# Two heads of an attention group side by side on TensorE: row tiles for the scores, column tiles for the value products

## The chip, the core and the metric

The kernel runs on one core of a Trainium2 chip. The metric is the device time of one execution in microseconds (us). The kernel before took 1734.57 us (median of three runs, 1733.45 to 1736.35).

## What is computed

Two layers of a diffusion trunk work on 128 context tokens and 512 latent tokens (a grid of 8 rows by 64 columns), 640 tokens of width 1024. Of a layer, this is the part that matters here:

```python
q, k, v = heads(da), heads(mla), heads(na)        # 4 heads of 64 per group
# differential attention (da):  p = softmax(q1 k1) - lam * softmax(q2 k2);  o = p v
# latent attention (mla):       p = softmax(q k / sqrt(96));                o = p v
# neighbourhood attention (na): a latent query sees 8 x 16 neighbours (bias rpb) and 128 context keys
s_loc = where(col_ok, q kb * scale + bias, -inf);  s_ctx = q kc * scale
p = softmax(concat(s_loc, s_ctx));                 o = p_loc vb + p_ctx vc
mixed = concat(o_da, o_mla, o_na, o_conv) @ w_out
x = x + g1 * mixed;   x = x + g2 * (relu(h @ w_ff1) ** 2 @ w_ff2)
```

Latent tokens read the 128 cached context keys and their own; context tokens read only themselves. The context's keys and values are outputs as well.

## The kernel before

The large products run as three fp32r products of split operands (`mm3`, lines 244 to 246: high by high, high by low, low by high). A weight granule of 512 KB comes in on the queue of SP (L214), and ACT and POOL split it (L192, L193). The attention itself runs in plain f32 on TensorE, where the trace shows two records (passes) for each matmul.

The attention of a layer is a pipeline of 60 units in the order neighbourhood, differential, latent: 20 units each, a unit being one head and one tile of 128 queries (four latent tiles i = 0 to 3 and the context tile i = 4). `PROGRAM` sets the stages of a unit: at step t its scores (`Sa`) and the row maximum (`ma`); two steps on the transposes of the probabilities (`T`, L686) and their copy to SBUF (`ev`, L692), after the exponential (`xa`) and the division by the row sum (`sc`) one step earlier or in the same step; three steps on the value products (`PV`, L697) and their split into high and low (`oc`, L192 and L193). Between the steps stand background pieces (`mm3` of the coming projections and of the output projection), spread by a list of first and last steps. A tile scheduler then fixes the order of each engine.

Neighbourhood units went head by head (h = 0 to 3, five tiles each). A head has 64 channels, and a pair of heads fills the 128 partitions of `q` and `k`: the scores of one unit use 64 partitions, three blocks of 128 keys (L756 to L758) or one (L750, the context tile). `u["s_"]` and `u["t"]` lie in one of three PSUM slots of 1024 f32 (`s`). The bias of a head has three tables of 128 x 384; each has its buffer, and the table of the next head is loaded behind the last use of this head's (L734).

The value products took the values of both heads of a pair as weights (128 columns) for each unit, and `o_split` kept the 64 output partitions of the unit's own head. The turned probabilities `pt` have two buffers of 2560 bytes a partition. `o` lies in one of two PSUM banks (`g`), which the background pieces use too.

Of the kernel before, what the change touches and what calls it, by code (L numbers as in the profile page):

```python
# [16 lines left out]
T = 640  # L17
# [65 lines left out]
class Builder:  # L83
# [462 lines left out]
    def v(self, name):  # L546
        return self.A("va" if name == "na" else "vb", 0, 6, 256)
# [140 lines left out]
    def turn_out(self, u):  # L688
        self.pti += 1
        n = u["nb"] * 128  # L690
        u["pt"] = self.A("pt", 2560 * (self.pti % 2), n)
        self.nc.scalar.copy(u["pt"], u["t"][:, 0:n])  # L692

    def pv(self, u, p, vals):
        u["o"] = self.g()[:, 0:128]
        for b, v in enumerate(vals):
            self.nc.tensor.matmul(u["o"], v[:, p * 128:p * 128 + 128] if v.shape[1] > 128 else v, u["pt"][:, b * 128:b * 128 + 128],  # L697
                                  start=b == 0, stop=b == len(vals) - 1)
# [5 lines left out]
    def o_split(self, u, h, i):  # L704
# [25 lines left out]
    def na_bias(self, kind):  # L730
        return self.F("e", 8192 + 1536 * kind, 384)

    def na_bias_load(self, l, h, kind):
        self.nc.sync.dma_start(self.na_bias(kind), self.d["nab"][l, h, kind])  # L734

    def na_unit(self, l, h, i, orow):
        nc = self.nc
        p, r0 = h // 2, 64 * (h % 2)
        rows = slice(r0, r0 + 64)
        q = self.qk_q("na", p)[rows, i * 128:i * 128 + 128]  # L740
        k = self.qk_k("na", p)[rows]
        v = self.v("na")
        nk = 128 if i == 4 else 384
        u = {"nb": nk // 128}

        def S():
            sl = self.slot()
            u["s_"], u["t"] = sl[:, 0:nk], sl[:, 640:1024]
            if i == 4:
                nc.tensor.matmul(sl[:, 0:128], q, k[:, 640:768], start=True, stop=True)  # L750
                return
            nxt, prv = 128 * min(i + 1, 3), 128 * max(i, 1) - 64
            step = abs(prv - nxt)
            lo = min(nxt, prv)
            pair = k[:, lo:lo + 2 * step].rearrange("p (a b) -> p a b", b=step)[:, ::-1 if prv < nxt else 1, 0:64]
            nc.tensor.matmul(sl[:, 0:128], q, pair, start=True, stop=True)  # L756
            nc.tensor.matmul(sl[:, 128:256], q, k[:, i * 128:i * 128 + 128], start=True, stop=True)
            nc.tensor.matmul(sl[:, 256:384], q, k[:, 512:640], start=True, stop=True)  # L758

        def mx():  # L760
            m = u["m"] = self.small()
            if i == 4:
                nc.vector.tensor_reduce(out=m, in_=u["s_"], axis=AX.X, op=ALU.max, negate=True)
            else:
                kind = (0, 1, 1, 2)[i]
                nc.vector.tensor_tensor_reduce(out=u["s_"], in0=u["s_"], in1=self.na_bias(kind), scale=-1.0,
                                               scalar=3e38, op0=ALU.add, op1=ALU.min, accum_out=m)
                if i != 1 and h < 3:
                    self.na_bias_load(l, h + 1, kind)

        def ex():
            s = u["s"] = self.small()
            u["e"] = self.F("e", 1536 * ((h * 5 + i) % 4), nk)
            nc.scalar.activation(u["e"], u["s_"], AF.Exp, bias=u["m"], scale=1.0 if i == 4 else -1.0, accum_out=s)

        return {
            "Sa": S, "ma": mx, "xa": ex, "sc": lambda: self.softmax_row(u, ROWS[l]), "T": lambda: self.turn(u),
            "ev": lambda: self.turn_out(u),
            "PV": lambda: self.pv(u, p, [v[:, 5]] if i == 4 else [self.edge(p)[:, i], v[:, i], v[:, 4]]),
            "oc": lambda: self.o_split(u, h, i),  # L780
        }

    def mla_unit(self, l, h, i, orow):
# [5 lines left out]
        u = {"nb": nk // 128}  # L789
# [19 lines left out]
        return {  # L809
            "Sa": S, "ma": mx, "xa": ex, "sc": lambda: self.softmax_row(u, ROWS[2 + l]), "T": lambda: self.turn(u),  # L810
            "ev": lambda: self.turn_out(u),
            "PV": lambda: self.pv(u, h // 2, [v[:, 5]] if i == 4 else [v[:, j] for j in range(5)]),
            "oc": lambda: self.o_split(u, h, i),
        }

    def stk(self, mm):
# [30 lines left out]
    def da_unit(self, l, h, i, orow):  # L847
        nc = self.nc
        v = self.v("da")
        st = [self.stk(2 * (h % 2) + c) for c in range(2)]  # L850
        nk = 128 if i == 4 else T
        sq = self.F("sq", 40 * (h // 2 % 2), 5, 2)
        u = {"nb": nk // 128}

        def S(c):
            if c == 0:
# [18 lines left out]
        def sc():  # L875
# [16 lines left out]
            "oc": lambda: self.o_copy(u, h, i, orow),  # L892
        }

    def pipeline(self, l, hooks):
        self.ei = 2
        order = [(self.na_unit, h, i) for h in range(4) for i in range(5)]
        order += [(self.da_unit, h, i) for h in range(4) for i in range(5)]
        order += [(self.mla_unit, h, i) for i in (0, 1, 2, 4, 3) for h in range(4)]
        rows = [self.F("conv", 5120 + 2560 * p, T) for p in range(2)]  # L900
        n = len(order)
        units = []
        depth = max(int(p[-1]) for p in PROGRAM if p != "|")
        for t in range(n + depth):
            if t < n:
                make, h, i = order[t]
                units.append(make(l, h, i, rows[h // 2]))
# [12 lines left out]
            if t in hooks:  # L920
                hooks[t]()
# [482 lines left out]
    def mix(self, l):  # L1404
        nc, d = self.nc, self.d
# [5 lines left out]
            self.in_conv(l, self.lead)  # L1411
        self.swap(l, "bt")
        self.lam(l)
        for kind in range(3):
            self.na_bias_load(l, 0, kind)
# [280 lines left out]
```

## Time and profile before

| what | value |
|---|---|
| median of three runs | 1734.57 us |
| the profiled execution, its own time | 1735.52 us |
| its span in the trace | 1733.6 us |
| TensorE (PE) busy | 1664.6 us, 96% |
| VectorE (DVE) busy | 1083.0 us, 62% |
| ScalarE (ACT) busy | 740.7 us, 43% |
| GpSimd (POOL) busy | 656.5 us, 38% |
| mean granted TensorE clock | 0.986 |

Busy shares are means over stages with different limits, so the page is read by stages. In layer 0 the neighbourhood units lie at about 156 to 262 us, the differential ones at 262 to 338, the latent ones at 338 to 405; layer 1 has the same at about 992 to 1105, 1105 to 1181 and 1181 to 1248. The time of a matmul on the busy line is its latency; what it costs a full engine is the step from its start to the next start, and that is read from the timeline.

### The profile page before, as it was taken

Reading aid. Unit: us, or ns where it says so; the run is one execution under the profiler, and the core shown is the slowest. Engines: PE = TensorE matmul, PEld = TensorE weight load, DVE = VectorE, ACT = ScalarE, POOL = GpSimd, SP = SyncE. Lnnn points to the kernel's source line nnn. Section 1 sums busy time; section 2 is a strip of 40 time slices with the busy share of each in tenths; the row PEclk is TensorE's granted clock in tenths of the full one; section 3 lists DMA queues with packets and bytes.
Section 4 is the critical chain, followed back from the end, with each engine's and each line's share of the span. In section 5 each row is a group of like instructions: output and inputs, shape, how many; then the busy total and the mean of one; then the engine's idle time right before and its main releaser. Section 6 shows DMA issues by size and latency. Waiting matters only on the chain. (4 is left out here: it accounts for less than half of the span.)

```text
span 1733.6 us, 29318 instructions
## 1 busy us (share of the span) xinstructions
PE 1664.6 (96%) x11368; PEld 1570.3 (91%) x11368; DVE 1083.0 (62%) x2136; ACT 740.7 (43%) x1655; POOL 656.5 (38%) x527
## 2 busy tenths in 40 slices
PE   7999999999989999999999899999999999999997
PEld 5869988788889999999999888887989999999997
DVE  4772448868988887876377933886784333333335
ACT  4323666756423332222343247776563322332322
POOL 0225533305344455544324364332343333333330
PEclk8999999999989999999999999999999999999999
DMA  9563244202355454443222222430113222222221
GB/s 367 185 202 106 75 110 101 63 14 86 110 160 167 147 158 147 152 153 111 73 71 71 64 86 84 108 88 20 50 39 97 73 74 74 80 79 74 74 62 61
DMA packets 62331, 178.28 MB, mean 103 GB/s; under 512 B 8656, under 2 KB 20048, under 8 KB 62192
## 3 DMA queue, kind: packets, MB, share of 16 engines
q1 hardware_dynamic: 61984, 176.14, 33.0%
q8 instruction: 89, 1.46, 0.3%
q14 instruction: 50, 0.41, 0.1%
q10 hardware_dynamic: 144, 0.13, 0.0%
q0 software_dynamic: 64, 0.14, 0.0%
HBM read 158.52 MB, written 3.83 MB: 94 GB/s over the span
## 5 line engine op out<-in xcount | busy, mean ns | idle before, releaser
L193 POOL TENSOR_TENSOR ra<-fa,ra 128x512 fp32r<-128x512 f32 (+1 forms) x239 | 345.7, 1459 | 545.2 <-ACT ra L192 524.5
L193 POOL TENSOR_TENSOR we<-fa,we 128x512 fp32r<-128x512 f32 x126 | 188.8, 1510 | 275.2 <-ACT we L192 253.5
L1077 DVE TENSOR_TENSOR fr<-fr 128x384 f32<-128x384 f32 (+1 forms) x128 | 103.9, 814 | 273.7 <-ACT or L1076 150.6
L192 ACT CAST ra<-fa 128x512 fp32r<-128x512 f32 (+1 forms) x240 | 147.2, 621 | 255.1 <-PE s L245 163.7
L244 PE MATMUL s<-ra 128*128 128x256 f32 (+2 forms) x600 | 185.4, 309 | 8.3 <-DVE fa L392 7.6
L245 PE MATMUL s<-ra 128*128 128x256 f32 (+2 forms) x600 | 184.3, 307 | 0.0
L246 PE MATMUL s<-ra 128*128 128x256 f32 (+2 forms) x600 | 184.1, 307 | 0.0
L301 DVE CUSTOM_DVE_ANT_0 fa<-fa 128x1024 f32<-128x1024 f32 x112 | 173.2, 1546 | 0.2
L392 DVE SCALAR_TENSOR_TENSOR fa<-s,fa 128x128 f32<-128x128 f32 (+1 forms) x310 | 121.3, 427 | 74.8 <-PE s L246 74.8
L246 PE MATMUL g<-ra 128*128 128x384 f32 (+2 forms) x508 | 158.3, 312 | 8.7 <-POOL ra L193 8.7
L244 PE MATMUL g<-ra 128*128 128x384 f32 (+2 forms) x508 | 162.2, 319 | 2.5 <-DVE bt L1010 1.9
L245 PE MATMUL s<-ra,we 128*128 128x384 f32 (+1 forms) x480 | 152.1, 317 | 12.0 <-DVE ra L370 12.0
L245 PE MATMUL g<-ra 128*128 128x384 f32 (+2 forms) x508 | 157.8, 311 | 0.8 <-POOL ra L193 0.8
L192 ACT CAST we<-fa 128x512 fp32r<-128x512 f32 x132 | 81.2, 620 | 175.2 <-PE s L245 127.9
L246 PE MATMUL s<-ra,we 128*128 128x384 f32 (+1 forms) x480 | 150.1, 313 | 0.0
L244 PE MATMUL s<-ra,we 128*128 128x384 f32 (+1 forms) x480 | 148.8, 314 | 0.8 <-DVE fa L520 0.8
L392 DVE SCALAR_TENSOR_TENSOR fa<-g,fa 128x128 f32<-128x128 f32 (+1 forms) x266 | 109.3, 441 | 40.4 <-PE g L246 39.0
L244 PEld LDWEIGHTS s<-ra 128*128 128x128 f32 x600 | 115.6, 193 | 17.6 <-DVE fa L392 7.9
L423 DVE SCALAR_TENSOR_TENSOR fa<-fa 128x670 f32<-128x670 f32 x120 | 124.1, 1098 | 0.5
L697 PE MATMUL g<-at 128*128 128x128 f32 x848 | 116.9, 277 | 2.8 <-DVE fa L392 1.5
L245 PEld LDWEIGHTS s<-ra 128*128 128x128 f32 x600 | 115.9, 193 | 4.0 <-issue 4.0
L246 PEld LDWEIGHTS s<-ra 128*128 128x128 f32 x600 | 115.8, 193 | 3.6 <-issue 3.6
(299 smaller groups left out, 4484.4 us busy)
## 6 DMA issues: line engine op xcount, KB each, us to landing
fa<-in_wg SPq DMA_DIRECT2D x187, 512.0 KB, 3.6
fa<-in_wmod SPq DMA_DIRECT2D x73, 512.0 KB, 4.2
at<-in_wmod SPq DMA_DIRECT2D x20, 512.0 KB, 6.5
ra<-ra SPq DMA_DIRECT2D x64, 96.0 KB, 2.2
ra<-ra SPq DMA_DIRECT2D x64, 80.0 KB, 2.3
fa<-in_nab SPq DMA_DIRECT2D x24, 192.0 KB, 3.7
fa<-in_xT SPq DMA_DIRECT2D x8, 320.0 KB, 5.9
os<-in_wmod SPq DMA_DIRECT2D x3, 512.0 KB, 10.2
```

The source lines that it names most:

```text
L192: nc.scalar.copy(hi, src)
L193: (lo_eng or nc.gpsimd).tensor_tensor(out=lo, in0=src, in1=hi.bitcast(F32), op=ALU.subtract)
L244: nc.tensor.matmul(out, a[0], b[0], start=start, stop=False)
L245: nc.tensor.matmul(out, a[0], b[1], start=False, stop=False)
L246: nc.tensor.matmul(out, a[1], b[0], start=False, stop=stop)
L301: self.nc.vector.tensor_tensor_reduce(out=self.junk, in0=slot, in1=self.cb[:, v], scale=1.0, scalar=0.0, op0=ALU.mult, op1=ALU.add, accum_ ...
L392: self.mark = nc.vector.scalar_tensor_tensor(out=xs, in0=ps[:, a - t0:b - t0], scalar=self.mod(l, v, which)[:, m:m + 1], in1=xs, op0=ALU.m ...
L423: nc.vector.scalar_tensor_tensor(out=y, in0=g[:, j:j + 670], scalar=dwh[:, c, j:j + 1], in1=y, op0=ALU.mult, op1=ALU.add)
L697: self.nc.tensor.matmul(u["o"], v[:, p * 128:p * 128 + 128] if v.shape[1] > 128 else v, u["pt"][:, b * 128:b * 128 + 128], start=b == 0, s ...
L1077: nc.vector.tensor_tensor(out=r, in0=r, in1=r, op=ALU.mult)
```

## The change

Units of neighbourhood attention now come in pairs of heads for each query tile. At the first unit of a pair the scores of both heads are issued, block by block and head by head, the heads on partitions 0 to 63 and 64 to 127 and into the two banks of one slot. The second unit issues none. In neighbourhood and latent attention the value products of both heads are issued at the second unit (`pv2`): 64 weight columns each, one head into output partitions 0 to 63, the other into 64 to 127 of one bank. Differential attention keeps `pv`. `o_split` runs once for a pair, on 128 partitions. The turned probabilities have three buffers (1536 bytes for neighbourhood units, 2560 for the others; the third of those lies over the edge values and a scratch row). The bias tables are read in the order of the pairs (number n = 0 to 11 for a layer) through the same three buffers, and table n + 3 is loaded behind the last use of table n.

```diff
-        u["pt"] = self.A("pt", 2560 * (self.pti % 2), n)
+        u["pt"] = self.A("pt", u["size"] * ((self.pti + 2) % 3), n)
...
+    def pv2(self, u):
+
+        u["o"] = self.g()[:, 0:128]
+        pair = (u["mate"], u)
+        for b in range(u["nb"]):
+            for c, w in enumerate(pair):
+                self.nc.tensor.matmul(u["o"][64 * c:64 * c + 64], w["v"](b), w["pt"][:, b * 128:b * 128 + 128],
+                                      start=b == 0, stop=b == u["nb"] - 1)
...
-        r, c = slice(64 * (h % 2), 64 * (h % 2) + 64), slice(i * 128, i * 128 + 128)
-        hi, lo = (self.R("ob", off, 2, T)[r, h // 2, c] for off in (0, 5120))
-        self.split(hi, lo, u["o"][r], self.nc.vector)
+        c = slice(i * 128, i * 128 + 128)
+        hi, lo = (self.R("ob", off, 2, T)[:, p, c] for off in (0, 5120))
+        self.split(hi, lo, u["o"], self.nc.vector)
...
+    def na_bias_load(self, l, n):
+        if n < 12:
+            self.nc.sync.dma_start(self.na_bias(n), self.d["nab"][l, n // 6 * 2 + n % 2, n // 2 % 3])
...
+            for b in range(nk // 128):
+                for r in range(2):
+                    rows = slice(64 * r, 64 * r + 64)
+                    q, k = self.qk_q("na", p)[rows, i * 128:i * 128 + 128], self.qk_k("na", p)[rows]
...
+                    at = 512 * r + 128 * b
+                    nc.tensor.matmul(sl[:, at:at + 128], q, k, start=True, stop=True)
...
-                if i != 1 and h < 3:
-                    self.na_bias_load(l, h + 1, kind)
+                if i != 1:
+                    self.na_bias_load(l, bias + 3)
...
-        order = [(self.na_unit, h, i) for h in range(4) for i in range(5)]
+        order = [(self.na_unit, 2 * p + c, i) for p in range(2) for i in range(5) for c in range(2)]
```

The scheduler's order follows. On PE of layer 0, late in the neighbourhood units where few background pieces stand, the kernel before has scores (L756 to L758), transposes (L686), value products (L697) and a sum over channels (L641) one unit after another:

```order
L686 MATMUL s_67<-fa 128x128 x3
L697 MATMUL g_63<-at_81,fa 128x128
L697 MATMUL g_63<-at_81 128x128 x2
L641 MATMUL g_64<-fa 128x384
L756 MATMUL s_67<-bt_636 128x128
L757 MATMUL s_67<-bt_636 128x128
L758 MATMUL s_67<-bt_636 128x128
L686 MATMUL s_65<-fa 128x128 x3
L697 MATMUL g_63<-at_81,fa 128x128
```

The changed kernel has there, on PE, the scores of a pair in one row of six (L781), the transposes of its two units apart, and the value products of a pair in six (L706):

```order
L781 MATMUL s_65<-bt_636 128x128 x6
L686 MATMUL s_67<-fa 128x128 x3
L706 MATMUL g_63<-at_81,fa 64x128 x2
L706 MATMUL g_63<-at_81 64x128 x4
L641 MATMUL g_64<-fa 128x384
L686 MATMUL s_67<-fa 128x128 x3
L781 MATMUL s_66<-bt_636 128x128 x6
L641 MATMUL g_63<-fa 128x256
```

Two visits to the scores became one, and so did two visits to the value products; the count of matmuls is the same.

Not all pairs stay whole. The fourth pair of layer 0 on PE, in the changed kernel, where L443 is the channel sum of the convolution's norm:

```order
L443 MATMUL g_63<-fa 128x512
L686 MATMUL s_65<-fa 128x128 x3
L781 MATMUL s_67<-bt_636 128x128
L443 MATMUL g_64<-fa 128x128
L781 MATMUL s_67<-bt_636 128x128
L686 MATMUL s_65<-fa 128x128 x3
L781 MATMUL s_67<-bt_636 128x128 x3
L706 MATMUL g_63<-at_81 64x128 x6
L244 MATMUL g_64<-ra 128x256
```

Its six score products stand in four places (the sixth follows behind the next 24 background products), so that some have nothing of the other head beside them.

## Rows read from the trace of the kernel before

**Rows 1.** The page's part 1: busy us, share of the span, instructions.
```profile
PE 1664.6 (96%) x11368; PEld 1570.3 (91%) x11368; DVE 1083.0 (62%) x2136; ACT 740.7 (43%) x1655; POOL 656.5 (38%) x527
```
**Rows 2.** Windows of layer 0: busy us (count) of PE, PEld, DVE, ACT, POOL; granted clock, DMA.
```profile
156.00:232.00 76.00, 75.70 (x511) 69.81 (x509) 27.98 (x95) 46.55 (x112) 38.91 (x40) 1.00 0.27 83
232.00:244.00 12.00, 11.15 (x73) 8.61 (x72) 6.47 (x19) 10.70 (x33) 5.40 (x4) 1.00 0.56 136
...
262.00:338.00 76.00, 70.36 (x490) 62.97 (x490) 67.70 (x143) 55.52 (x142) 28.31 (x35) 1.00 0.33 82
338.00:405.00 67.00, 66.66 (x453) 57.72 (x452) 45.81 (x107) 39.62 (x99) 11.95 (x10) 1.00 0.10 34
```
**Rows 3.** PE passes of single lines: count, ns min/median/max, first and last start.
```profile
L697 PE MATMUL g<-at x848: 271/275/378, 175.5 to 1257.6; 128*128 128x128 f32 x170
...
L697 PE MATMUL g<-at,fa x32: 271/275/377, 229.0 to 1105.1; 128*128 128x128 f32 x32
...
L756 PE MATMUL s<-bt x64: 272/272/373, 156.6 to 1085.0; 64*128 64x128 f32 x64
...
L750 PE MATMUL s<-bt x16: 272/322/373, 176.5 to 1088.7; 64*128 64x128 f32 x16
```
**Rows 4.** Timeline of PE, layer 0: start us, us, line, out<-in, weights, moving, count.
```profile
184.74 0.36 PE L244 MATMUL g<-ra 128*128 128x256 f32 x1
...
184.95 0.28 PE L245 MATMUL g<-ra 128*128 128x256 f32 x1
...
185.06 0.28 PE L246 MATMUL g<-ra 128*128 128x256 f32 x1
...
187.69 0.83 PE L697 MATMUL g<-at 128*128 128x128 f32 x6
...
227.33 0.33 PE L245 MATMUL g<-ra 128*128 128x384 f32 x1
227.50 0.34 PE L246 MATMUL g<-ra 128*128 128x384 f32 x1
227.77 0.48 PE L756 MATMUL s<-bt 64*128 64x128 f32 x2
228.10 0.38 PE L757 MATMUL s<-bt 64*128 64x128 f32 x2
228.32 0.38 PE L758 MATMUL s<-bt 64*128 64x128 f32 x2
228.63 0.55 PE L686 MATMUL s<-fa 128*128 128x128 f32 x3
```
**Rows 5.** Timeline of PE at the start: L1263 writes four column groups in turn.
```profile
47.22 0.34 PE L244 MATMUL s<-ra,wes 128*128 128x384 f32 x1
47.49 0.62 PE L1263 MATMUL s<-at,fa 128*2 128x128 f32 x16
48.04 0.44 PE L245 MATMUL s<-ra,wes 128*128 128x384 f32 x1
48.32 0.34 PE L246 MATMUL s<-ra,wes 128*128 128x384 f32 x1
```
**Rows 6.** Timeline of PE: 512 moving columns, two column groups (L1358), full array (L458).
```profile
88.31 1.05 PE L1358 MATMUL g<-fa 128*32 128x512 f32 x4
...
193.81 1.02 PE L458 MATMUL g<-fa 128*128 128x512 f32 x2
```
**Rows 7.** ACT groups by form: count, busy us, mean ns, idle before.
```profile
L192 ACT CAST or<-g 64x128 fp32r<-64x128 f32 x80 | 20.7, 258 | 21.7 <-PE g L697 20.8
...
L774 ACT ACTIVATE fa<-s,fa 128x384 f32<-128x384 f32 x32 | 18.7, 585 | 26.2 <-DVE fa L766 25.8
```
**Rows 8.** SP's queue: the page's DMA issues (count, KB, us to landing), weight issues.
```profile
fa<-in_nab SPq DMA_DIRECT2D x24, 192.0 KB, 3.7
...
167.75 0.33 SPq L214 DMA_DIRECT2D fa<-in_wg  x1
...
177.43 0.33 SPq L214 DMA_DIRECT2D fa<-in_wg  x1
```

More of the change, by code (lines that the diff above doesn't have):

```diff
@@ L696, in pv @@
         for b, v in enumerate(vals):
-            self.nc.tensor.matmul(u["o"], v[:, p * 128:p * 128 + 128] if v.shape[1] > 128 else v, u["pt"][:, b * 128:b * 128 + 128],
+            self.nc.tensor.matmul(u["o"], v[:, p * 128:p * 128 + 128], u["pt"][:, b * 128:b * 128 + 128],
                                   start=b == 0, stop=b == len(vals) - 1)
+    def pv2(self, u):
[5 more added lines that the diff above has]
+                                      start=b == 0, stop=b == u["nb"] - 1)
     def o_copy(self, u, h, i, row):
@@ L702, in o_copy, with o_split @@
         self.nc.scalar.copy(row[r, i * 128:i * 128 + 128], u["o"][r])
[L704 to L707 removed]
+    def o_split(self, u, p, i):
+        c = slice(i * 128, i * 128 + 128)
+        hi, lo = (self.R("ob", off, 2, T)[:, p, c] for off in (0, 5120))
+        self.split(hi, lo, u["o"], self.nc.vector)
     def softmax_row(self, u, on_act):
@@ L728, in edge_load, with na_bias, na_unit, v @@
         nc.sync.dma_start(e[64:128, 0:1], v[64:128, 0:1])
[L730 to L736, printed above, removed]
-        nc = self.nc
[L738 to L742, printed above, removed]
-        nk = 128 if i == 4 else 384
-        u = {"nb": nk // 128}
+    def na_bias(self, n):
+        return self.F("e", 8192 + 1536 * (n % 3), 384)
+    def na_bias_load(self, l, n):
+        if n < 12:
+            self.nc.sync.dma_start(self.na_bias(n), self.d["nab"][l, n // 6 * 2 + n % 2, n // 2 % 3])
+    def na_unit(self, l, h, i, mate):
+        nc = self.nc
+        p, c = h // 2, h % 2
+        val = self.v("na")
+        nk = 128 if i == 4 else 384
+        bias = 6 * p + 2 * (0, 1, 1, 2, 0)[i] + c
+        u = {"nb": nk // 128, "mate": mate, "size": 1536}
+        def v(b):
+            cols = slice(64 * h, 64 * h + 64)
+            if i < 4 and b == 0:
+                return self.edge(p)[:, i, 64 * c:64 * c + 64]
+            return val[:, 5 if i == 4 else (i, 4)[b - 1], cols]
+        u["v"] = v
         def S():
[L747 to L750, printed above, removed]
+            if c:
+                u["s_"] = u["t"] = mate["sl"][:, 512:512 + nk]
                 return
+            sl = u["sl"] = self.slot()
+            u["s_"] = u["t"] = sl[:, 0:nk]
             nxt, prv = 128 * min(i + 1, 3), 128 * max(i, 1) - 64
@@ L754, in S @@
             lo = min(nxt, prv)
[L755 to L758, printed above, removed]
+            for b in range(nk // 128):
+                for r in range(2):
+                    rows = slice(64 * r, 64 * r + 64)
+                    q, k = self.qk_q("na", p)[rows, i * 128:i * 128 + 128], self.qk_k("na", p)[rows]
+                    if i == 4:
+                        k = k[:, 640:768]
+                    elif b == 0:
+                        k = k[:, lo:lo + 2 * step].rearrange("p (a b) -> p a b", b=step)[:, ::-1 if prv < nxt else 1, 0:64]
+                    else:
+                        k = k[:, i * 128:i * 128 + 128] if b == 1 else k[:, 512:640]
+                    at = 512 * r + 128 * b
+                    nc.tensor.matmul(sl[:, at:at + 128], q, k, start=True, stop=True)
         def mx():
@@ L764, in mx @@
             else:
-                kind = (0, 1, 1, 2)[i]
-                nc.vector.tensor_tensor_reduce(out=u["s_"], in0=u["s_"], in1=self.na_bias(kind), scale=-1.0,
+                nc.vector.tensor_tensor_reduce(out=u["s_"], in0=u["s_"], in1=self.na_bias(bias), scale=-1.0,
                                                scalar=3e38, op0=ALU.add, op1=ALU.min, accum_out=m)
-                if i != 1 and h < 3:
-                    self.na_bias_load(l, h + 1, kind)
+                if i != 1:
+                    self.na_bias_load(l, bias + 3)
         def ex():
             s = u["s"] = self.small()
-            u["e"] = self.F("e", 1536 * ((h * 5 + i) % 4), nk)
+            u["e"] = self.F("e", 1536 * ((i * 2 + c) % 4), nk)
             nc.scalar.activation(u["e"], u["s_"], AF.Exp, bias=u["m"], scale=1.0 if i == 4 else -1.0, accum_out=s)
@@ L778, in na_unit, with mla_unit @@
             "ev": lambda: self.turn_out(u),
-            "PV": lambda: self.pv(u, p, [v[:, 5]] if i == 4 else [self.edge(p)[:, i], v[:, i], v[:, 4]]),
-            "oc": lambda: self.o_split(u, h, i),
+            **({"PV": lambda: self.pv2(u), "oc": lambda: self.o_split(u, p, i)} if c else {}), "u": u,
         }
-    def mla_unit(self, l, h, i, orow):
+    def mla_unit(self, l, h, i, mate):
         nc = self.nc
@@ L811, in mla_unit @@
             "ev": lambda: self.turn_out(u),
-            "PV": lambda: self.pv(u, h // 2, [v[:, 5]] if i == 4 else [v[:, j] for j in range(5)]),
-            "oc": lambda: self.o_split(u, h, i),
+            **({"PV": lambda: self.pv2(u), "oc": lambda: self.o_split(u, h // 2, i)} if h % 2 else {}), "u": u,
         }
@@ L906, in pipeline @@
                 make, h, i = order[t]
-                units.append(make(l, h, i, rows[h // 2]))
+                units.append(make(l, h, i, rows[h // 2] if make == self.da_unit else units[-1]["u"] if h % 2 else None))
             for p in PROGRAM:
@@ L1413, in mix @@
         self.lam(l)
-        for kind in range(3):
-            self.na_bias_load(l, 0, kind)
+        for n in range(3):
+            self.na_bias_load(l, n)
         self.in_v(l, "na")
```

6 lines of the change are left out of this document (3 added, 3 removed).

## The prediction, before the result was known

> **What bounds the kernel now.** I read the busy line first, then the windows by stage, then the timeline of PE. PE is busy for 96% of the span [rows 1], and by stage it is PE that is full where the change works: 75.70 of 76 us in the neighbourhood stage and 66.66 of 67 in the latent one, at the full granted clock [rows 2]. Two stretches are less clear. In the thin one at 232 to 244 us, where few background pieces stand, PE has 11.15 us of 12 and ACT 10.70, so ACT is right behind. In the differential stage DVE has 67.70 of 76 and PE 70.36; the change adds and removes next to nothing there, so I expect no gain from it. Busy time is latency, so prices come from steps between starts.
>
> One f32 pass of 128 moving columns costs a full PE 0.11 us: six value passes last 0.83 us with one of them 0.275, so (0.83 - 0.275) / 5 = 0.11; two score passes go from 228.10 to 228.32, again 0.11 each [rows 3, 4]. A matmul is two passes, 0.22 us. A visit to 64-row scores costs more than its passes. From the last background start to the first score start it is 0.27 us where the step before was 0.17, so 0.10 to get in; from 227.77 to the transposes at 228.63 it is 0.86 for six passes worth 0.66 [rows 4]. That is 0.30 us for each visit.
>
> **The scores.** The trace has 64 passes on each of L756, L757 and L758 (one of the three lines stands) and 16 on L750: 208 passes, 104 matmuls [rows 3]. Before: 208 x 0.11 = 22.9 us, and 42 visits in the scheduler's order at 0.30 = 12.6; together 35.5. After, counted in the order of the changed kernel: 28 visits instead of 20, because pairs are cut in some places, and of the 104 matmuls 92 stand as 46 pairs of opposite heads next to each other, 12 alone. If the two row halves run side by side: 46 x 0.22 + 12 x 0.22 + 28 x 0.30 = 10.1 + 2.6 + 8.4 = 21.1, a saving of 14.4 us. If they run in turn: 22.9 + 8.4 = 31.3, a saving of 4.2. Nothing in the trace has two row halves next to each other, so these are the two ends. The nearest row is of column groups: L1263 puts sixteen passes of 128 moving columns into four column groups, and from 47.49 to the next start at 48.04 they take 0.55 us [rows 5]; in turn they would be 16 x 0.11 = 1.76. Four turns of 0.11 and 0.11 to get out fit. I take the side-by-side end, since the row halves also have separate PSUM banks in this change. The Trainium skill, page "TensorE: Matmul & The Clock Gate", section "The mechanism", says that matmuls at different row groups overlap too; no run here shows it.
>
> **The value products.** 848 + 32 passes are 440 matmuls [rows 3]: 104 neighbourhood (2 layers, 4 heads, 4 x 3 + 1 blocks), 168 differential, 168 latent (4 x 5 + 1 blocks). The change pairs 272. Before: 272 x 0.22 = 59.8 us with no entry price, as they use the full array. After: 136 pairs at 0.22 if the column halves run side by side, 29.9, with 0.4 for two cut pairs, and 42 visits. A visit's price is read at L1263: in 0.27 - 0.17 = 0.10, out 0.55 - 0.44 = 0.11 [rows 4, 5]: 42 x 0.21 = 8.8. The long first step behind it (48.04 to 48.32) is not new: behind value products of the full array the first fp32r step is long too, 0.21 from 184.74 to 184.95, where the next one takes 0.11 [rows 4, 5]. Together 39.1, a saving of 20.7 us.
>
> The differences from L1263 are 64 weight columns instead of 2. L1358 is between: four passes of 512 moving columns with 32 weight columns in two groups take 1.05 us to the end of the last, as two passes of the full array do, 1.02 [rows 6]. So loads of 32 columns hide. At 64 columns the upper end is that they don't hide at all, and the halves then run in turn: 59.8 + 8.8, 8.8 us more than before. I take the value from the rows. A rule of the Trainium skill speaks against it: the same section says that "LDWEIGHTS overlaps with in-flight MATMULs only when row_grp differs". Column halves use all rows, so by that rule the halves would run in turn; rows 5 and 6 differ from it, and the measurement decides.
>
> **The rest.** `o_split` runs 40 times on 128 partitions instead of 80 times on 64, which leaves ACT 40 x 0.26 = 10 us [rows 7] and DVE about the same; neither is the bound in the full stages, so this counts at nothing. Fewer value products take one of the two shared PSUM banks, and a third buffer for the turned probabilities lets a copy run ahead; a pair needs it, since the first head's copy is held until the second's is made. I count both at nothing (at most 2 us of gain). The second unit's row maximum comes at once behind the first's, so exponentials and divisions stand in twos on ACT: the first unit waits another 0.59 us [rows 7]; in the full stages 24 or more background products stand between scores and transposes, which hide it.
>
> **What is given back.** In the thin stretch about five units lie. PE would drop by 5 x (14.4 + 6.8) / 40 = 2.7 us to 8.5 (6.8 is the neighbourhood share of the value saving: 22.9 - 11.4 - 22 x 0.21). ACT drops by 5 / 2 x 0.26 to about 10.0 [rows 2, 7], and becomes the bound. If it were then full, the 12 us become 10.0; if it keeps its share of 89%, 11.3. So 0.7 to 2.0 us a layer are lost again, and I take 2.0. Another 1 us a layer I leave for units in twos. That is an allowance, not a row.
>
> Sum: 14.4 + 20.7 - 6.0 = 29.1 us less. The profiled execution took 1735.5 by its own time (span 1733.6); 1706.4. The median of the runs lies 0.95 below it, so I forecast **1705.5 us**.
>
> **Rivals.**
> Row halves in turn. For it: no row shows them overlapping. The saving shrinks to 4.2 + 20.7, less 4 given back: 20.9, so 1713.7.
> The softmax chain takes over. ACT and DVE, not PE, pace the neighbourhood units once PE is lighter. For it: the thin stretch. Against: ACT has 46.55 of 76 us in the full part [rows 2]. If two thirds of the neighbourhood gain of 21.2 are lost, 14, in place of the 6 above: 21.1 less, and with a third of the latent gain of 13.9 gone too, 16.5 less: 1713 to 1718.
> Column halves in turn. Scores save 14.4, value products cost 8.8: 5.6 less, 1729. Against: rows 5 and 6.
> Slower: bias tables come late. A table now is loaded three units ahead (before, four or five), and four tables a layer are of this tight kind; some 14 units lie in the first 76 us [rows 2], 5.4 us a unit, so two pairs' scores are about 10.8 us apart. The load lands 3.7 us after its issue, but SP's queue is in order and weight loads that wait for POOL's split stand in it, 9.7 us apart [rows 8]. If every tight table were held for a whole such turn, it would be 9.7 + 3.7 - 10.8 = 2.6 us late; behind two turns, 12.3. DVE's row maximum would wait at the head of its queue, and exponentials, transposes and the next scores behind it. Eight tables late by 5 us are 40 us against 29: 1745. It decides from 3.6 us each. Against it: the scheduler puts two tables in a row right behind the first pair's maxima.
>
> **How the numbers follow.** Side by side in both: 0.69. Row halves in turn: 0.12. Chain: 0.10. Column halves in turn: 0.04. Late tables: 0.05. The range takes in the full saving with nothing given back and 2 us of relief, 1735.5 - 37.1 - 0.95 = 1697, and the chain rival, 1718. A measurement of this kernel tells about 0.2%, 3.5 us, from no change. Faster by more than that: the first three and most of the fourth, with a little off for unread waits, 0.91. Within: 0.04. Slower: 0.05.
>
> **What would show it.** Passes of the two heads in the scores start within a few ns of each other, pairs 0.11 apart: right; 0.11 between heads: the first rival. The same in the value products for the third. PE still above 95% in 156 to 225 us with the stage about 10 us shorter; the latent stage about 7 us shorter; the differential stage unchanged. PE's idle time ended by ACT or DVE in the neighbourhood stage would show the chain; DVE's maxima waiting for the bias DMA the late tables. Wrong altogether would be a step from visit to visit above 0.3 us for changing the tile shape.

## The result

The changed kernel takes 1715.01 us (median of four runs, 1712.34 to 1716.02), the kernel before 1735.46 beside it: a ratio of 0.988, 95% interval 0.9863 to 0.9897. Measured again in the experiments it took 1714.21 us, ratio 0.9873 (0.9858 to 0.9889). The forecast was 1705.5 with a range of 1697 to 1718, so sign and range held, but some 20 to 22 us were gained and not 29 or 30. The question of this part is where the difference went. Medians are of undisturbed runs; the profiled executions of two experiments below, e5 and e6, were disturbed ones with spans of 1743.5 and 1751.1 us, so only single visits at the full clock are read from them.

The page's part 1 of the changed kernel answers [rows 1]; its profiled execution took 1712.34 us by its own time, with a span of 1710.1:

```profile
PE 1635.6 (96%) x11368; PEld 1530.5 (89%) x11368; DVE 1072.1 (63%) x2096; ACT 726.9 (43%) x1615; POOL 655.0 (38%) x527
```

Windows of layer 0 in the changed kernel (busy us and count of PE, PEld, DVE, ACT, POOL; granted clock, DMA share, GB/s), against [rows 2]: the full neighbourhood part, the thin stretch, the differential and the latent stage.

```profile
157.40:225.00 67.60, 67.42 (x498) 61.85 (x498) 26.12 (x89) 43.94 (x104) 39.16 (x40) 1.00 0.29 89
225.00:238.00 13.00, 9.79 (x83) 7.08 (x82) 5.61 (x20) 10.53 (x30) 5.01 (x4) 1.00 0.64 146
242.80:329.10 86.30, 81.19 (x562) 72.47 (x561) 75.08 (x158) 62.04 (x159) 34.81 (x40) 1.00 0.38 92
329.10:402.70 73.60, 71.57 (x530) 57.86 (x529) 50.44 (x112) 43.19 (x102) 17.41 (x14) 1.00 0.15 51
```

In the thin stretch TensorE now has 9.79 us of 13, where it had 11.15 of 12. The stages, from the first score product of one to the first of the next (the latent stage to the first product of the feed-forward part), read off the timelines of TensorE in us, one profiled execution each (NA is neighbourhood, DA differential attention); the experiments below are in the table too:

| kernel | NA, layer 0 | DA | latent | NA, layer 1 | DA | latent | six together |
|---|---|---|---|---|---|---|---|
| before | 95.2 | 86.4 | 77.7 | 106.2 | 86.4 | 77.9 | 529.9 |
| changed | 85.5 | 86.3 | 73.6 | 100.2 | 86.2 | 73.6 | 505.4 |
| changed, a second execution (e0) | 85.2 | 86.2 | 73.6 | 98.2 | 86.2 | 73.6 | 503.1 |
| order alone (e11) | 96.4 | 94.1 | 77.8 | 105.7 | 93.6 | 77.6 | 545.2 |
| order, row halves (e2) | 91.6 | 92.4 | 77.8 | 103.0 | 93.5 | 77.6 | 535.9 |
| order, column halves (e3) | 89.3 | 88.7 | 73.6 | 101.5 | 88.7 | 73.6 | 515.5 |
| changed, table 11 early (e1) | 83.3 | 87.8 | 73.6 | 95.0 | 88.0 | 73.6 | 501.3 |
| e1, division on DVE (e7) | 83.2 | 89.3 | 73.6 | 94.1 | 89.2 | 73.9 | 503.3 |
| e1, whole pairs (e8) | 81.9 | 89.0 | 73.6 | 93.3 | 87.8 | 73.7 | 499.3 |
| e1, pieces earlier (e9) | 79.7 | 93.8 | 75.7 | 90.6 | 95.0 | 75.7 | 510.4 |
| e1, both (e10) | 79.1 | 91.0 | 73.6 | 90.4 | 90.9 | 73.6 | 498.6 |

Of the 24.5 us that the profiled execution gained here, 9.7 and 6.1 are in the neighbourhood stages and 4.1 and 4.3 in the latent ones; the differential ones did not move. The rest of the program took 1203.7 us before and 1204.7 after.

Two cautions for this table. The two executions of the changed kernel agree within 0.3 us in all columns but the neighbourhood stage of layer 1, which differs by 2.0 us, and the rest of the program differs by 3.7 us between them (1204.7 and 1208.4). The border between two stages can move, too. In every kernel with the order in pairs, 12 records of the output projection that stood ahead of the first differential score stand behind it, and 4 value passes went the other way (in e9 and e10 more crossed): by their steps some 1.3 us of work left the neighbourhood column for the differential one in each layer.

**The halves do run side by side.** A pair's score visit on the timeline of TensorE (start, duration, form, count):

```profile
216.46 0.28 PE L246 MATMUL g<-ra 128*128 128x256 f32 x1
216.67 0.94 PE L781 MATMUL s<-bt 64*128 64x128 f32 x12
217.53 0.55 PE L686 MATMUL s<-fa 128*128 128x128 f32 x3
```

Twelve passes of two heads take 0.86 us to the next start, as the six of one head did [rows 4]; the entry is 0.21 where the step before was 0.12. And the value products of a latent pair:

```profile
344.47 1.31 PE L706 MATMUL g<-at 128*64 128x128 f32 x20
345.71 0.49 PE L819 MATMUL s<-bt 96*128 96x128 f32 x2
```

Twenty passes take 1.24 us; in turn at the 0.11 read from [rows 4] they would take 2.2. The Trainium skill, page "TensorE: Matmul & The Clock Gate", section "The mechanism", says that a weight load overlaps matmuls in flight only at another row group. Both halves use all rows here, so by that rule they would run in turn; the 1.24 us differ from it, and the measurement decides.

Summed over all visits (entry, and first start to the start behind the last, without waits), the scores went from 35.2 to 21.2 us and the paired value products from 60.2 (32 visits of 0.67, 32 of 1.10, 16 of 0.22) to 39.9. The prediction had 35.5 to 21.1 and 59.8 to 39.1. What TensorE does for the two terms was right within 1 us each, 34.3 us less; it is the path that did not get shorter by as much.

**A late table.** The thin stretch of layer 0 in the changed kernel (idle time and its releaser in brackets; SPq are SP's DMA issues, L788 is the row maximum, L744 the load of a bias table, L214 that of a weight granule):

```profile
226.96 0.57 DVE L788 CUSTOM_DVE_ANT_0 s<-s,fa 128x384 f32<-128x384 f32 x1 [1.56 <-PE s L781]
228.28 1.27 POOL L193 TENSOR_TENSOR ra<-fa,ra 128x512 fp32r<-128x512 f32 x1
229.58 0.33 SPq L214 DMA_DIRECT2D fa<-in_wg  x1
230.56 0.53 SPq L744 DMA_DIRECT2D fa<-in_nab  x1
234.57 0.62 PE L641 MATMUL g<-fa 128*128 128x256 f32 x2
235.34 0.57 DVE L788 CUSTOM_DVE_ANT_0 s<-s,fa 128x384 f32<-128x384 f32 x1 [3.08 <-DMA fa<-in_nab]
236.87 0.28 DVE L193 TENSOR_TENSOR or<-g,or 128x128 fp32r<-128x128 f32 x1
237.21 0.44 PE L244 MATMUL g<-or,ra 128*128 128x384 f32 x1 [2.02 <-DVE or L193]
```

Read it from the end. TensorE's next product (L244) waits 2.02 us for the low half of a split (L193 on VectorE), which frees its PSUM bank. That split stands in VectorE's queue behind a row maximum that waits 3.08 us for bias table 11. The table's buffer was free at 227.53 (226.96 + 0.57), but SP's queue stood at a weight load until POOL's split ended at 229.55; the table's load went out at 230.56 and landed some 4.7 us later. Layer 1 has the same, and worse. Two lines of TensorE's timeline there:

```profile
1066.13 0.69 PE L244 MATMUL g<-or,ra 128*128 128x384 f32 x1 [2.91 <-DVE or L193]
1066.61 0.52 PE L245 MATMUL g<-or,ra 128*128 128x384 f32 x1
```

And the windows of the wait and of the stretch behind it, columns as above:

```profile
1062.80:1066.10 3.30, 0.41 (x2) 0.01 (x1) 1.85 (x8) 1.19 (x4) 0.00 (x0) 0.82 0.70 157
1066.10:1072.60 6.50, 6.47 (x31) 6.12 (x33) 2.34 (x7) 3.35 (x11) 0.00 (x0) 0.57 0.64 143
```

TensorE was busy for 0.41 of 3.3 us, and the clock granted in the next 6.5 us was 0.57 of full, so most of it went at the lower level (1.2 GHz). From L244 to the first differential score it is 8.1 us here, 5.6 in layer 0.

### The profile page after: what moved, and what is told of

It reads as the page before. It is cut to its first block, busy times and chain, and to the rows that moved or that the text cites. A ratio compares the mean times of both kernels' runs of the same rounds, so it can differ in the third digit from the quotient of the medians.

```text
span 1710.1 us, 29240 instructions
## 1 busy us (share of the span) xinstructions
PE 1635.6 (96%) x11368; PEld 1530.5 (89%) x11368; DVE 1072.1 (63%) x2096; ACT 726.9 (43%) x1615; POOL 655.0 (38%) x527
## 5 line engine op out<-in xcount | busy, mean ns | idle before, releaser
L193 POOL TENSOR_TENSOR ra<-fa,ra 128x512 fp32r<-128x512 f32 (+1 forms) x239 | 346.1, 1461 | 504.2 <-ACT ra L192 467.0
L193 POOL TENSOR_TENSOR we<-fa,we 128x512 fp32r<-128x512 f32 x126 | 187.8, 1501 | 285.9 <-ACT we L192 261.5
L244 PE MATMUL s<-ra 128*128 128x256 f32 (+2 forms) x608 | 186.3, 307 | 1.4 <-DVE fa L1200 0.7
L392 DVE SCALAR_TENSOR_TENSOR fa<-s,fa 128x128 f32<-128x128 f32 (+1 forms) x310 | 121.3, 428 | 73.6 <-PE s L246 73.5
L245 PE MATMUL s<-ra,we 128*128 128x384 f32 (+1 forms) x472 | 150.2, 318 | 12.2 <-DVE ra L370 12.1
L244 PE MATMUL g<-ra 128*128 128x384 f32 (+2 forms) x500 | 160.8, 322 | 0.4 <-ACT fa L655 0.4
L244 PE MATMUL s<-ra,we 128*128 128x384 f32 (+1 forms) x472 | 147.5, 316 | 1.2 <-ACT ra L379 0.9
L246 PE MATMUL s<-ra,we 128*128 128x384 f32 (+1 forms) x472 | 148.2, 314 | 0.0
L244 PEld LDWEIGHTS s<-ra 128*128 128x128 f32 x608 | 115.4, 190 | 10.7 <-issue 7.4
L244 PE MATMUL g<-or,ra 128*128 128x256 f32 (+1 forms) x322 | 109.3, 339 | 5.4 <-DVE or L193 4.9
```

The costliest lines, as they stand in the source:

```text
L193: (lo_eng or nc.gpsimd).tensor_tensor(out=lo, in0=src, in1=hi.bitcast(F32), op=ALU.subtract)
L244: nc.tensor.matmul(out, a[0], b[0], start=start, stop=False)
L245: nc.tensor.matmul(out, a[0], b[1], start=False, stop=False)
L246: nc.tensor.matmul(out, a[1], b[0], start=False, stop=stop)
L392: self.mark = nc.vector.scalar_tensor_tensor(out=xs, in0=ps[:, a - t0:b - t0], scalar=self.mod(l, v, which)[:, m:m + 1], in1=xs, op0=ALU.m ...
```

## The experiments

The times are medians; the ratios are to the kernel before beside them (1736.2 to 1736.5 us). A ratio's interval is about 0.0015 to either side, some 2.7 us.

**The changed kernel again, and table 11 in its own place.** 

> The changed kernel once more, beside the three below on the same chip, so that their differences are read against it. Both theories: the ratio to the kernel before is 0.988, some 1715 us, and the step from the last channel sum to the first output-projection product near 235 us and near 1063 us shows waits of about 2.0 and 2.9 us.

> Bias table 11 of each layer gets a place of its own and is loaded one pair of heads earlier, behind table 10; all else is the changed kernel. Theory 'late table': in both layers VectorE waits about 3 us for this table, the low half of the output operand stands behind it in VectorE's queue, and TensorE waits 2.0 us (layer 0) and 2.9 us (layer 1) for that; in layer 1 the clock then falls and the next stretch takes 8.1 us instead of 5.6. All three go, 2.0 + 2.9 + 2.5 = 7.4 us, of which up to 3 may come back as the next wait: 1708 to 1711 us. Theory 'softmax chain': ScalarE is nearly full there (10.5 of 13 us), so the same time is spent waiting for exponentials: 1714 to 1716 us.

```diff
-        return self.F("e", 8192 + 1536 * (n % 3), 384)
+        return self.F("e", 6144 if n == 11 else 8192 + 1536 * (n % 3), 384)
...
-                    self.na_bias_load(l, bias + 3)
+                    [self.na_bias_load(l, n) for n in {7: (10, 11), 8: ()}.get(bias, (bias + 3,))]
```

In e1 table 11 is loaded three units earlier than in the changed kernel. Measured: 1714.21 us for the changed kernel, 1708.96 with the table early, ratio 0.9843 (0.9827 to 0.9859), in the range of the first theory. In the second execution of the changed kernel VectorE's waits for the table are 2.86 and 3.17 us. TensorE's are 1.8 us in layer 0, where 2.0 was expected, and 2.1 in layer 1, where 2.9 was expected; the way from L244 to the first differential score is 7.0 us there and not 8.1, with the clock at 0.74 in the 6.5 us from 1065.20. So the size of the second wait and of what follows it varies from execution to execution. The same place on the timeline of e1:

```profile
232.17 0.57 DVE L788 CUSTOM_DVE_ANT_0 s<-s,fa 128x384 f32<-128x384 f32 x1 [0.72 <-ACT fa L796]
233.76 0.62 PE L641 MATMUL g<-fa 128*128 128x256 f32 x2
233.81 0.29 DVE L193 TENSOR_TENSOR or<-g,or 128x128 fp32r<-128x128 f32 x1
234.16 0.44 PE L244 MATMUL g<-or,ra 128*128 128x384 f32 x1
```

The maximum no longer waits for the table, and L244 starts 0.40 us behind L641 instead of 2.64. The late table is shown by the wait that is gone. Its price is less sure: the medians say 5.2 us, and the two intervals just touch. The neighbourhood columns are 2.2 and 5.2 us shorter than in the first execution of the changed kernel, 1.9 and 3.2 than in the second, and the differential stage takes 1.5 and 1.8 back. So the six stages show 4.1 or 1.8 us; the rest of the 5.2 lies where nothing was changed. The wait for ScalarE that the rival put here (L686 for L723) is 0.6 us in both kernels.

**One part at a time.** 

> Row halves alone: the scores stay in pairs, the value products and their splits are done unit by unit on the full array as in the kernel before. Theory 'late table': by the rows of the two traces the paired value products save 20.8 us and all of that is on the path; it is 20.8 slower than the changed kernel, 1734 to 1737 us. Theory 'softmax chain': in the neighbourhood stage the value products' saving was already lost to ScalarE and VectorE, so only the latent share of 14 comes back: 1728 to 1731 us.

> Column halves alone: value products in pairs, but each unit issues its own scores, so no row halves stand next to each other. Theory 'late table': the scores' saving of 14.0 us by the rows is gone, 1727 to 1730 us. Theory 'softmax chain': the scores' saving was partly lost already to ScalarE, so undoing it costs 7 us or less: 1720 to 1723 us.

> Only the order in pairs of heads: the units, tables, slots and third buffer of the changed kernel, but each unit issues its own scores and its own value products on the full array, so nothing stands side by side. It tells apart why row halves alone were 4.3 us slower than the kernel before although their rows save 5.0 us a layer (17.6 to 12.6). Theory 'the order in twos costs some 14 us, and only the column halves with one PSUM bank a pair pay it back': without the row halves 10 us more, 1748 to 1753 us. Rival 'the row halves' saving never reached the path, since units in twos wait for banks and splits': 1739 to 1743 us.

Row halves alone (e2) do value products and splits by unit:

```diff
-            **({"PV": lambda: self.pv2(u), "oc": lambda: self.o_split(u, p, i)} if c else {}), "u": u,
+            "PV": lambda: self.pv(u, p, [val[:, 5]] if i == 4 else [self.edge(p)[:, i], val[:, i], val[:, 4]]),
+            "oc": lambda: self.o_half(u, h, i), "u": u,
```

Column halves alone (e3) let each unit issue its own scores, into its half of the pair's slot:

```diff
-                for r in range(2):
+                for r in (c,):
```

`o_half` is the split of the kernel before, and the latent units are changed in the same way; e11 has both edits. Measured: order alone 1752.91 us (ratio 1.0095, 1.0078 to 1.0111); order and row halves 1740.67 (1.0024, 1.0015 to 1.0032); order and column halves 1724.32 (0.9927, 0.9914 to 0.9941). All four kernels together make a ledger:

| step | without the other | with the other |
|---|---|---|
| order in pairs, nothing side by side | +16.5 | |
| row halves | -12.2 (1752.9 to 1740.7) | -10.1 (1724.3 to 1714.2) |
| column halves | -28.6 (1752.9 to 1724.3) | -26.5 (1740.7 to 1714.2) |

For e2 and e3 no theory held as it was put: both lie outside what either had said. One reason for e3 is seen: VectorE's wait for bias tables, 6.0 us in the changed kernel measured beside it, is 0.5 us there, so it was spared a part of the late table. For e2, the rows say that row halves save 5.0 us a layer against e11 (visits of 17.7 and 12.6 us), and they were worth 12.2 in the time: they did reach the path, and e11's first theory held. So it is the order that costs, with what belongs to it: the paired slots and tables and the third buffer. The late table is no part of the 16.5: VectorE waits for no table in e11, 2.1 us in e2 and 6.0 in the changed kernel, so its price stands in the steps of the ledger that end at the changed kernel.

Where it costs is seen in the stage table: +1.2 and -0.5 us in the neighbourhood columns, +7.7 and +7.2 in the differential ones. With the 1.3 us that crossed the border, some 2.5 and 0.8 belong to the neighbourhood units and 6.4 and 5.9 to the differential stage. The window of that stage in the kernel before, then in the order-alone kernel, and one of a stretch within it:

```profile
251.70:338.10 86.40, 79.78 (x552) 71.61 (x551) 76.16 (x159) 62.67 (x158) 34.28 (x40) 1.00 0.36 88
253.00:347.10 94.10, 82.97 (x561) 75.06 (x560) 79.82 (x162) 63.70 (x161) 34.05 (x40) 0.96 0.33 81
276.20:284.00 7.80, 4.58 (x21) 4.02 (x22) 6.95 (x11) 4.39 (x12) 3.68 (x4) 0.67 0.56 141
```

Of the 7.7 us 4.5 are idle time of TensorE (11.1 against 6.6) and 3.2 are busy time, with the 1.3 us of work from across the border and at a lower mean clock. The granted clock of this stage is 1.00 in both layers of the other kernels of the table, but for 0.98 in layer 0 of e8, and below it in both layers of the three that are longest there: e11 (0.96 and 0.96), e2 (0.98 and 0.96) and e9 (0.98 and 0.96).

A wait inside the stretch from 276.20 to 284.00, on the timeline of TensorE and VectorE:

```profile
278.66 0.34 PE L246 MATMUL g<-ra 128*128 128x384 f32 x1
280.55 0.56 DVE L1034 COPY bt<-g 64x384 f32<-64x384 f32 x1
281.16 0.69 PE L244 MATMUL g<-ra 128*128 128x384 f32 x1 [2.16 <-DVE bt L1034]
```

TensorE waits 2.16 us for VectorE to empty a PSUM bank, and the clock is at 0.67 in the window around it. The row-halves kernel has the wait too (2.1 us); in the kernel before the same wait is 1.0 us. In the thin stretch a value product there waits in the same way for the split of another (order with row halves, timeline):

```profile
239.05 0.70 PE L641 MATMUL g<-fa 128*128 128x256 f32 x2
240.42 0.57 DVE L793 CUSTOM_DVE_ANT_0 s<-s,fa 128x384 f32<-128x384 f32 x1 [0.57 <-DMA fa<-in_nab]
241.08 0.29 DVE L193 TENSOR_TENSOR or<-g,or 64x128 fp32r<-64x128 f32 x1
241.43 0.49 PE L697 MATMUL g<-at,fa 128*128 128x128 f32 x2 [1.67 <-DVE or L193]
```

With column halves a pair takes one of the two shared banks and one split, not two. That fits the 6 to 8 us by which they bring more than their 20.3 us on the engine; it is seen in these waits, not tried by itself. Longer waits and the lower clock behind them are what the differential stage shows; why the order brings them, when the units of that stage are the same, the runs leave open.

**A third buffer alone.** 

> The kernel before with nothing but a third buffer for the turned probabilities (1536 bytes in neighbourhood units, 2560 in the others). Theory 'relief counts for nothing': copies were not what TensorE waited for, 1734 to 1737 us. Rival 'the buffer carries part of the gain': copies run ahead and 3 us or more go, 1732 us or less.

```diff
-        u["pt"] = self.A("pt", 2560 * (self.pti % 2), n)
+        u["pt"] = self.A("pt", (1536 if "na" in u else 2560) * ((self.pti + 2) % 3), n)
```

Measured: 1738.38 us, ratio 1.0012 (1.0003 to 1.0021). This lies above the ranges of both theories, and the interval lies above 1: by itself the buffer brings nothing and costs some 2 us, for a reason that the runs leave open. It is there because a pair needs it.

**In turn.** 

> The kernel with bias table 11 in its own place, with one loop turned round: a pair's scores run head by head (A1 A2 A3 B1 B2 B3) and not block by block (A1 B1 A2 B2 A3 B3); every engine's order is otherwise the same. Theory 'the overlap is the gain': only A3 and B1 still stand side by side, so each of the 16 three-block pairs takes two matmuls more, 16 x 2 x 0.22 = 7.0 us: 1715 to 1717 us. Rival 'row halves gain by the visits alone': no change, 1708 to 1710 us. Rival 'TensorE is not the bound there any more': a part of the 7.0 is hidden, 1711 to 1714 us.

> The kernel with bias table 11 in its own place, with the two loops of the paired value products turned round: all blocks of one head, then all of the other, in the same place, bank and split. Theory 'the overlap is the gain': of a three-block pair 2 and of a five-block pair 4 matmuls of 0.22 us come back, 16 x 2 x 0.22 + 16 x 4 x 0.22 = 21.1 us: 1727 to 1731 us. Rival by the rule that loads overlap matmuls only at another row group: column halves ran in turn already, no change, 1708 to 1710 us. Against the kernel with row halves alone (1740.7 us), which has the value products' passes in full too but a PSUM bank and a split for each unit, the distance to this kernel is what the one bank and one split of a pair are worth: near 10 us by the first theory, none if only passes count.

```diff
-            for b in range(nk // 128):
-                for r in range(2):
+            for r in range(2):
+                for b in range(nk // 128):
```

For the columns:

```diff
-        for b in range(u["nb"]):
-            for c, w in enumerate(pair):
+        for c, w in enumerate(pair):
+            for b in range(u["nb"]):
```

Measured: row halves in turn 1714.58 us, ratio 0.9868 (0.985 to 0.9887), 5.6 more than e1; column halves in turn 1722.55, 0.9915 (0.99 to 0.9931), 13.6 more. A score visit with rows in turn, on TensorE's timeline:

```profile
217.79 1.26 PE L781 MATMUL s<-bt 64*128 64x128 f32 x12
218.99 0.55 PE L686 MATMUL s<-fa 128*128 128x128 f32 x3
```

A latent value visit with columns in turn:

```profile
346.84 2.02 PE L706 MATMUL g<-at 128*64 128x128 f32 x20
348.79 0.49 PE L819 MATMUL s<-bt 96*128 96x128 f32 x2
```

A score visit takes 1.20 us instead of 0.86, a latent value visit 1.95 instead of 1.24, and a three-block one 1.07 instead of 0.81. 14 x 0.33 (from the unrounded starts) = 4.6 us for the rows (14 pairs are whole) and 16 x 0.71 + 14 x 0.26 = 15.0 for the columns: the measured 5.6 and 13.6 agree within their intervals, and the rivals with no change fall. The expected 7.0 and 21.1 were too much, since even then the halves overlap more than one matmul (below). The last comparison that was expected of e6 is with e2. There e6 is 18.1 us faster, of which 5.3 are passes (60.2 against 39.9 + 15.0) and at most 5.2 the late table. That leaves some 8 us or more for one bank, one split and whatever else the pairing of the value products changes; the expected 10 fits.

**Attempts on what is left.** All four rest on e1.

> The kernel with bias table 11 in its own place; the neighbourhood units' division by the row sum runs on VectorE and not on ScalarE, 0.6 us less on ScalarE for each unit. Theory 'ScalarE's chain of two units is what is left of the give-back in the thin stretch': the wait of the transposes for it (0.77 us near 232.5 and 1060) goes and the stretch gets 1 to 2 us shorter in each layer, 1705 to 1707 us. Rival 'the chain is as long on VectorE, whose queue also holds maxima that wait': no gain, 1709 to 1713 us.

> The kernel with bias table 11 in its own place; the second to the sixth score product of a pair get a higher priority in the scheduler, so that no pair is cut: 20 visits instead of 28, 52 pairs and none alone. Theory 'a visit and a single product cost what the rows say': in each layer the two cut pairs now take five visits of 0.41 us and one of 0.64 with six entries of 0.10, 3.3 us, and whole they take 0.87 + 0.36 + 0.20, 1.4 us: 1.9 us less a layer, 3.7 in all, 1704 to 1707 us. Rival 'TensorE is not the bound where pairs are cut': 1708 to 1710 us.

> The kernel with bias table 11 in its own place; the first output-projection pieces begin two units earlier (step 16 instead of 18), so that six to twelve background products stand in each gap of the thin stretch. Theory 'what is left of the give-back is waits in the thin stretch': the waits of 0.75 and 0.77 us for GpSimd and ScalarE there in each layer are covered, 2 to 4 us less in all, 1705 to 1707 us. Rival 'the pieces are only moved, and lack where the differential stage needs them': 1708 to 1711 us.

> Table 11 in its own place, whole pairs and the earlier background pieces together. Theory 'the three costs are independent': the gains of the two runs above add up to 5 to 8 us, 1701 to 1704 us, below both kernels. Rival 'what one frees the differential stage takes back, with VectorE at 67.7 of 76 us there': no better than the better of the two, 1705 us or more.

The edits of e7, e8 and e9, in this order; e10 has those of e8 and e9:

```diff
-ROWS = (1,1,0,0)
+ROWS = (0,0,0,0)
```

```diff
-                    nc.tensor.matmul(sl[:, at:at + 128], q, k, start=True, stop=True)
+                    with self.later(-400 if b or r == 1 else 0):
+                        nc.tensor.matmul(sl[:, at:at + 128], q, k, start=True, stop=True)
```

```diff
-PL = (0, 15, 22, 24, 27, 26, 34, 34, 41, 46, 59, 25, 28, 58, 63, 18, 23)
+PL = (0, 15, 22, 24, 27, 26, 34, 34, 41, 46, 59, 25, 28, 58, 63, 16, 23)
```

Measured: e7 1711.3 us (0.9859, 0.9844 to 0.9874), e8 1708.8 (0.9844, 0.9831 to 0.9857), e9 1716.23 (0.9884, 0.987 to 0.9898), e10 1707.14 (0.9832, 0.9819 to 0.9846). Against the 1708.96 of e1 only e9 is clearly off, and it is slower, outside both of its theories; e7, e8 and e10 came out in the ranges of their rivals. The stage table says why. e7 takes the wait for ScalarE away and shortens the neighbourhood stages by 0.1 and 0.9 us; the differential ones get 1.5 and 1.2 longer. e8 shortens the visits by some 1.8 us a layer, near what the rows said (10.6 to 8.8), the neighbourhood stages by 1.4 and 1.7, and layer 0, with the clock at 0.98, hands 1.2 back; in the times nothing is seen. e9 shortens the neighbourhood stages by 3.6 and 4.4 and lengthens the differential ones by 6.0 and 7.0 and the latent ones by 2.1. The window of the differential stage of layer 0 in e1:

```profile
239.90:327.60 87.70, 81.44 (x560) 72.34 (x559) 76.00 (x157) 61.87 (x159) 34.90 (x40) 1.00 0.38 91
```

The same stage in e9:

```profile
237.20:331.00 93.80, 84.05 (x567) 74.01 (x566) 76.53 (x158) 64.75 (x165) 35.30 (x40) 0.98 0.38 93
```

VectorE has 76 us of work in either. The moved pieces do not lack in this stage by count: 198 records of the output projection lie ahead of the next stage and behind the first differential score in both kernels. What crossed the border are 12 value passes, 6 transposes and 4 channel-sum records of the last neighbourhood units, some 2.4 us of TensorE's steps, so that much of the shorter column is work put off. All three stages of a layer together are 4.5 and 4.7 us longer. TensorE's idle time in the differential stage grows from 6.3 to 9.8 us, and the clock falls there; what makes the waits longer is open. e10 is the best version of this study and beats both kernels: its interval lies below that of the changed kernel (0.9858 to 0.9889). That it beats e1 is not shown.

## Why the prediction was right, and where it was wrong

**Scores, 14.4 us: right.** Both heads' passes run side by side, 0.86 us a visit, 35.2 to 21.2 us on the rows. In the time they were worth 10.1 to 12.2, with the order in pairs charged apart.

**Value products, 20.7 us: right on the engine, short in the time.** 42 visits, 39.9 us where 39.1 was said. The price of a visit came out near 0.24 us, not 0.21: 1.24 - 10 x 0.11 = 0.14 inside and at the exit, and an entry of 0.10. But the path gained 26.5 to 28.6. The surplus fits the PSUM banks and splits that the prediction counted at nothing (at most 2 us); it was seen in waits, not tried by itself. The third buffer brought nothing, as was said; alone it cost 2 us.

**What is given back, 6.0 us: the step that failed.** It was one allowance for a full ScalarE and another, without a row, for units in twos. The order in pairs alone costs 16.5 us. 16.5 - 12.2 - 26.5 = -22.2: that is the result, where the prediction's sum was 6.0 - 14.4 - 20.7 = -29.1. The mechanism of the two savings was right and this term was mis-sized by 10.5 us. On this way through the ledger the column halves made 5.8 good and the row halves fell 2.2 short. That an allowance too small by 10.5 met a surplus nobody had counted is luck, and it kept the time within the range. The late table's price is hidden in the last of these steps. Why the order costs 16.5 us stays open; the runs show longer waits and a lower clock in the differential stage.

**The cause of the thin stretch was the wrong one.** ScalarE was taken as the next bound there. Taking its work away (e7) changed nothing in the time. What stood behind the longest waits was the rival "bias tables come late", thought of as eight tables and 40 us: it struck one table a layer, 2.0 and 2.9 us of TensorE's time in one execution and 1.8 and 2.1 in the other, with the lower clock behind the second, 5.2 us by the medians. Its mechanism was as written there, a load behind a weight load that waits for POOL's split. The mistake was to price it as all or nothing, and to weigh it with a chance instead of counting it for the last table, whose pair follows at once in the thin stretch.

**By stage.** "About 10 us shorter" held in layer 0 (9.7), though some 1.3 of it only crossed the border. Layer 1 got 3.6 less; with the table early the two layers gain 11.9 and 11.2, so most of the 3.6 is the table and the clock behind it. "PE still above 95%" in the full part held (67.42 of 67.6 us). The latent stage was to be 7 us shorter and was 4.1 and 4.3. Waits of TensorE by line in the latent stage of layer 0 (us in total, times, longest), in the changed kernel:

```profile
PE s L686 <- DVE fa L725: 0.9, 2, 0.6
PE g L245 <- POOL or L193: 0.7, 1, 0.7
PE g L706 <- DVE fa L392: 0.4, 1, 0.4
```

In the kernel before:

```profile
PE g L244 <- DVE or L193: 0.3, 1, 0.3
PE s L686 <- DVE fa L716: 0.3, 1, 0.3
```

That is 2.0 us where 0.6 was. The first of two score products takes 0.10 us longer in six places where it did in two, 0.4 us more; the ten visits at 0.24 are another 0.3. Four more records of the output projection stand ahead of the stage's end (162 against 158), 4 x 0.12 = 0.5. The last 0.2 of the 2.8 I can't place. "The differential stage unchanged" held for this kernel in its length, with 1.3 us of work more in it, but not as a rule: with nothing side by side it is 7 us longer, in e1 it gives back 3.3 of 7.4 us saved ahead of it, in e10 6.1 of 8.8, and in e7 and e9 more than was saved. It was the one stage of [rows 2] where VectorE and TensorE stood close to each other, and a saving upstream should have been weighed against it.

**Median and profile.** Of the distance from 1705.5 to 1715.0, 4.6 us are the sum of the stages (24.5 gained, 29.1 said); most of the rest is that the profiled execution of the changed kernel is the fastest of its four runs, 2.7 us under their median.

## What to carry to other kernels

Before you pair units to share an engine, run the new order with nothing shared: here it cost 16.5 us, much more than was allowed for it, and most of it showed up a stage later than the code that was changed. Where stages are compared, count what each of them holds, since work can cross the border. When an engine gets lighter, list each load with its lead in time and with the waits that stand ahead of it in its queue; one table a layer loaded three units earlier was worth some 5 us by the medians. A saving ahead of a stage that two engines fill about equally is not banked until that stage has been seen with it.

## What the runs showed of the hardware

Two column halves overlap even when the program issues one after the other. In the visit of 20 passes above, all ten of one head are issued first; the records have a second chain of starts that begins at 347.55, beside the seventh pass of the first chain, whose last three start at 347.66, 347.77 and 347.88 in between. So passes of the later half start ahead of passes issued earlier, and the visit takes 1.95 us instead of 20 x 0.11 + 0.14 = 2.3. The row halves do the same: the second head's first pass comes with the first head's third, and a visit takes 1.20 us. The records do not name the head. A half's first pass is known by its length: 323 ns for the values and 373 for the scores, where the later ones take some 272. Such passes stand at the head of the visit and at 347.55, with seven passes ahead of the second, so three of the first ten must start behind it; which of the later starts are theirs is read from the steps alone.

The loads of 64 weight columns take 132 to 137 ns in the records and still leave 0.11 us from pair to pair; loads of two halves that use all rows overlap each other and the matmuls of the other half.
